# One pool for raw weights, split weights and activations; expert chunks split five ahead; the gated activation split half way through the next products

## The chip, the cores and the metric

The program runs as one launch on one core of a Trainium2 chip. The core has four compute engines with their own instruction queues, TensorE (PE, with its weight loads shown apart as PEld), VectorE (DVE), ScalarE (ACT) and GpSimd (POOL), a queue engine SyncE (SP) that issues the loads here, and DMA engines that move the data. The metric is the device time of the launch in microseconds (us).

## The reference

A two-layer encoder over 256 frames of width 1024, in float32. Each layer adds a token mixer (a convolution of 31 taps, a gated convolution of 3 taps, a spatial gating block), a cross-attention to 256 memory tokens, and a feed-forward: dense in layer 0, a mixture of experts in layer 1. Cut to the last, which takes most of the time:

```python
def moe_swiglu(xn, w_router, w_gate, w_up, w_down):
    xt = xn.reshape(-1, d)                                   # 256 tokens
    top_vals, top_idx = lax.top_k((xt @ w_router), 2)        # 2 of 8 experts
    top_w = jax.nn.softmax(top_vals, axis=-1)
    combine = jnp.sum(one_hot(top_idx, 8) * top_w[..., None], axis=1)
    for e in range(8):                                       # 1024 -> 3584 -> 1024
        y = y + combine[:, e:e + 1] * (silu(xt @ w_gate[e]) * (xt @ w_up[e])) @ w_down[e]
```

A final RMS norm follows.

## The kernel before

**Products in float32 by parts.** A weight is loaded as float32 (a *raw* tile `w`, 128x2048, 1 MiB, called a chunk here) and split: ACT copies it to a tile `hi` of the type that PE multiplies fast (L195), DVE subtracts to get the rest `lo` (L196). Activations are split in the same way, and a product is the sum of three: hi with hi, hi with lo, lo with hi (`mm3`, L216). The class `Stream` (L149) holds the sequence of chunks. `get` (L203) hands out the next split half-chunk; before that it splits as far ahead as `SPLIT_AHEAD = 3` half-chunks and `SPLIT_BUFS = 3` chunks allow, and each split issues the load of the chunk `ahead` places on. In the expert stage `wide` is set, and a whole chunk is split by one ACT and one DVE instruction. With these numbers, when PE is handed chunk k, chunk k+2 is split.

**The pools.** Tiles `hi` and `lo` come from a pool `hp` of 3 buffers each. Raw chunks and the large activations come from a pool `rp` of `R_BUFS = 16` buffers of 8 KB per partition; the expert stage loads `R_BUFS - 7 = 9` chunks ahead of the split (L1378). Small tiles come from `mp`. A buffer is written again when its last reader is done.

**The order.** Each engine runs its instructions in the order in which the code emits them. Buffers are assigned when the program is built.

**The expert stage** (`moe`, `Run.blocks`, `Block`). The experts are sorted by their number of tokens: eight places, four *large* (128 token slots) and four *small* (64 slots). A place has 7 blocks of 512 hidden columns, 56 blocks in all. `merged` (L1325) puts three large blocks first, then small and large in turn 25 times, then three small ones. A block has two chunks for the gate product, two for the value product and two for the down product, 336 chunks in all. A chunk takes 12 matmuls of 512 columns in a large block (all three products), 8 in a small one (hi and lo of the 64 slots share one 128-wide weight). For each block `b` and the block `prev` before it, `Run.blocks` emits:

1. `b.gate()`: two chunks, then ACT reads the result (a large block: Silu, L1235; a small one: a copy, L1213).
2. `prev.hidden()`: PE turns the gated activation of the block before (L1225 large, L1223 small); for a small block DVE multiplies gate and value (L1256); then ACT and DVE split it into `hl` (L1262, L1263).
3. `b.value()`: two chunks, then DVE multiplies by the gate (large, L1243) or ACT copies (small).
4. `b.gated()`: for a small block PE turns the gate and ACT takes the Silu (L1249).
5. `prev.down()`: two chunks against `hl` of the block before (PE tile `acc`; the gate and value products are PE tile `mm` from `xg`).

So from one small block's down product to the next there are 12 chunks: small down 2, small gate 2, small value 2, large down 2, large gate 2, large value 2. Such a stretch is called a pair here. Between these, `pe_later` works off the gathering of the next place's tokens (L1146) and the adding of a finished place to the residual (L1175 to L1177).

**Kept chunks.** In layer 1 the first products of the attention's keys are done from chunks that were loaded and split during the dense feed-forward of layer 0 (`KEPT = 2`, `keep_load`, `keep_split`); each holds two blocks of 1024 columns. The last two key blocks are multiplied unsplit in float32 (L460).

Of the kernel before, what the change touches and what calls it, by code (L numbers as in the profile page):

```python
# [21 lines left out]
F32R = mybir.dt.float32r  # L22
# [40 lines left out]
SPL = [(j * 512, min(512, FF - j * 512)) for j in range((FF + 511) // 512)]  # L63


KEPT = 2

R_BUFS = 16
M_BUFS = 8

SPLIT_BUFS = 3
SPLIT_AHEAD = 3

HALF = 64
SMALL = 4
# [5 lines left out]
def trunk(tc, x, xt_in, mem, mt_in, wa, wb, wc, wl0, wk1, wl1, wff, wmoe, cc, tk, moec, ident_d, gfin, out):  # L81
    nc = tc.nc
    PE, ACT, DVE, POOL = nc.tensor, nc.scalar, nc.vector, nc.gpsimd
    with contextlib.ExitStack() as c:
# [1 line left out]
        cp = c.enter_context(tc.tile_pool(name="cp", bufs=1))  # L86
        rp = c.enter_context(tc.tile_pool(name="rp", bufs=R_BUFS))
        mp = c.enter_context(tc.tile_pool(name="mp", bufs=M_BUFS))
        hp = c.enter_context(tc.tile_pool(name="hp", bufs=SPLIT_BUFS))
        sp = c.enter_context(tc.tile_pool(name="sp", bufs=SMALL_BUFS))  # L90
        pp = c.enter_context(tc.tile_pool(name="pp", bufs=8, space=bass.MemoryType.PSUM))
        n_ = [0]
# [1 line left out]
        def nm(s):  # L94
            n_[0] += 1
            return f"{s}{n_[0]}"
# [52 lines left out]
        class Stream:  # L149
# [28 lines left out]
            def do_split(self):  # L178

                c, j, w, full = self.parts[self.ns]  # L180
                self.dma(c + 1)
                if full:
                    self.split[self.ns] = self.raw[c][:, j * w:(j + 1) * w]
                    self.ns += 1
                    self.dma(c + self.ahead)
                    return
                n = len(self.src[c][2])
                if c not in self.tiles:
                    self.tiles = {c: (hp.tile([P, n * w], F32R, name=nm("hi"), tag="hi"),
                                      hp.tile([P, n * w], F32R, name=nm("lo"), tag="lo"))}  # L190
                hi, lo = self.tiles[c]
                m = n - j if self.wide else 1
                ws = slice(j * w, (j + m) * w)
                r = self.raw[c][:, ws]
                ACT.activation(hi[:, ws], r, AF.Copy)  # L195
                DVE.tensor_tensor(lo[:, ws], r, hi[:, ws].bitcast(F32), op=OP.subtract)  # L196
                for i in range(j, j + m):
                    ws = slice(i * w, (i + 1) * w)
                    self.split[self.ns] = hi[:, ws], lo[:, ws]
                    self.ns += 1  # L200
                self.dma(c + self.ahead)

            def get(self, held=0):  # L203

                i = self.i
                c0 = self.parts[i - held][0]
                while (self.ns < min(i + 1 + SPLIT_AHEAD, len(self.parts))
                       and self.parts[self.ns][0] < c0 + SPLIT_BUFS):
                    self.do_split()
                self.i += 1  # L210
                return self.split.pop(i)
# [627 lines left out]
        def up(st, s, accs, mid=None):  # L839


            np_ = s.w // 128
            per = 1024 // s.w

            def part(i, wh, wl, t):
                for j in range(per):
                    k = i * per + j
                    w = slice(j * s.w, (j + 1) * s.w)
                    a, b = s.x(k, t)
                    mm3(accs[t][:, 0:s.w], a, b, wh[:, w], wl[:, w], k == 0, k == KC - 1)  # L850

            if mid:
                parts = st.many(np_)
                for t in range(NT):
                    for i in range(np_):
                        part(i, *parts[i], t)
                        if t == 0 and i == np_ // 2 - 1:
                            mid()
            else:
                for i in range(np_):  # L860
                    w = st.get()
                    for t in range(NT):
                        part(i, *w, t)
# [322 lines left out]
        class Block:  # L1186
# [13 lines left out]
                for i, (a, w) in enumerate(ops):  # L1200
                    PE.matmul(out, a, w, start=first and i == 0, stop=last and i == len(ops) - 1)  # L1201

            def up(self, out):
                for c in range(2):
                    items = []
                    for i, (wh, wl) in enumerate(self.st.many(2)):
                        items += [(4 * c + 2 * i + q, wh[:, q * 512:(q + 1) * 512], wl[:, q * 512:(q + 1) * 512])
                                  for q in range(2)]
                    self.product(self.place.xg, out, items, c == 0, c == 1)
# [24 lines left out]
                    self.a = M([P, 512], s="a")  # L1234
                    ACT.activation(self.a, g, AF.Silu)  # L1235

            def value(self):
                u = mm()
                self.up(u)
                if self.small:  # L1240
                    self.u = self.copy(u)
                else:
                    DVE.tensor_tensor(self.a, u, self.a, op=OP.mult)  # L1243
# [5 lines left out]
                    ACT.activation(self.a, ps, AF.Silu)  # L1249

            def hidden(self):
                n = self.place.n
                if self.small:
                    ps = self.turn(self.u)
                    self.hl = M([P, 4, 2, n], F32R, s="hl")
                    DVE.tensor_tensor(self.a, ps, self.a, op=OP.mult)  # L1256
                    v = self.a.rearrange("p (f s) -> p f s", f=4)
                else:
                    v = self.turn(self.a).rearrange("p (f s) -> p f s", f=4)
                    self.hl = R([P, 4, 2, n], F32R, s="hl")  # L1260
                hi, lo = self.hl[:, :, 0], self.hl[:, :, 1]
                ACT.activation(hi, v, AF.Copy)  # L1262
                DVE.tensor_tensor(lo, v, hi.bitcast(F32), op=OP.subtract)  # L1263
# [18 lines left out]
        class Run:  # L1282
# [14 lines left out]
            def blocks(self, st, steps, before):  # L1297

                fin = Final()
                prev = None  # L1300
                todo = [Block(st, p, j) for p, j in steps]
                for i, b in enumerate(todo):
                    last = i == len(todo) - 1
                    if i in before:
                        before[i]()
                    if last:
                        fin.load()
                    b.gate()
                    pe_later()
                    if prev:  # L1310
                        prev.hidden()
                    pe_later()
                    b.value()
                    pe_later()
                    b.gated()
                    if prev:
                        prev.down(b.hidden if last else None)
                    pe_later()
                    prev = b
                while later:  # L1320
                    pe_later()
                table(AF.Sqrt)
                prev.down(end=lambda: fin.all(prev.place.part))
# [35 lines left out]
        def moe(st, routed, weights, sort, combine):  # L1359
            slot, comb, slotp, combp, which, bases, nmax, r, saved = routed  # L1360
            where["tile"] = which
            order = merged()
            run = Run(slotp, combp, r, saved)
            places = [Place(run, p, 1 <= p <= SMALL) for p in range(NE)]

            places[0].run = Run(slot, comb, r, saved)
            st.wide = True
            first = places[0].gather()
            later.append(first.pop())
            later.append(combine)  # L1370
            for i, f in enumerate(first):
                f()
                if i == 0:
                    for _ in range(2):
                        st.do_split()
                    weights()
                    sort()
            st.ahead = R_BUFS - 7  # L1378
            before = {}
            at = {x: i for i, x in enumerate(order)}  # L1380

            def add(i, f):
                before.setdefault(i, []).append(f)
            add(LEAD, run.save)
            for p in range(1, NE):
                add(max(1, at[p, 0] - 3), places[p].prepare)
            run.blocks(st, [(places[p], j) for p, j in order],
                       {i: lambda fs=fs: [f() for f in fs] for i, fs in before.items()})

        def moe_rest(routed):  # L1390

            slot, comb, slotp, combp, which, bases, nmax, r, saved = routed
            here = T([P, NT, NE])
            DVE.tensor_tensor(here, slot, bases.unsqueeze(1).to_broadcast([P, NT, NE]), op=OP.subtract)
            run = Run(here, comb, r, saved)
            places = [Place(run, p, False) for p in range(NE)]
            order = [(p, j) for p in range(NE) for j in range(NJ)]
            st = Stream(chunks(order, lambda p, i: wmoe[p, i]), R_BUFS - 7)
            st.wide = True
            for f in places[0].gather():  # L1400
                f()
            run.blocks(st, [(places[p], j) for p, j in order],
                       {NJ * p - 1: places[p].prepare for p in range(1, NE)})
# [55 lines left out]
        norm = mixer(1, st, kv1, norm, start1)  # L1459
        nxt = Norm(1, C_FFN, split=False)  # L1460
        attention(1, st, kv1, norm, nxt)
        st.ahead = R_BUFS - 2
        routed, *pieces = route(nxt)
        moe(st, routed, *pieces)

# [147 lines left out]
```

## Time and profile before

| | |
|---|---|
| Median of 3 runs | 1571.79 us (1569.81 to 1572.13) |
| Profiled execution | 1567.52 us, span of its instructions 1565.7 us |
| PE busy | 1499.6 us (96%) |
| PEld busy | 1252.6 us (80%) |
| DVE busy | 1300.0 us (83%) |
| ACT busy | 1053.0 us (67%) |
| Data moved | 459.03 MB, mean 293 GB/s |

The expert stage takes the time from about 590 us to the end: 336 of the loads, 347 GB/s over that stretch. Before it PE is busy for 581.04 of 590 us. A busy share of PE is not a share at its peak: matmuls follow each other closer than one takes, and their ends are modelled, so short waits between two matmuls stand within the busy time. They are seen from the starts in a timeline.

### The profile page before, as it was taken

What the parts mean: (1) busy time and instruction counts of PE and PEld (TensorE: products, weight loads), DVE (VectorE), ACT (ScalarE), POOL (GpSimd) and SP (SyncE); (2) the same over time, 40 slices, a digit from 0 to 9 for tenths busy, and PEclk for the clock granted to TensorE, in tenths of its full rate; (3) what the DMA queues carried; (4) which work ended last, traced back from release to release, by engine and by line L of the source; (5) the groups of instructions that cost most, each with busy time, mean ns of one, the idle gap of its engine ahead of it and who ended that gap; (6) DMA issues with size and microseconds to landing.
All of it is one profiled execution on the core that took longest, in us unless ns stands there. A gap on an engine that the chain in (4) does not pass through costs nothing.

```text
span 1565.7 us, 20799 instructions
## 1 busy us (share of the span) xinstructions
PE 1499.6 (96%) x7757; PEld 1252.6 (80%) x7757; DVE 1300.0 (83%) x1496; ACT 1053.0 (67%) x1224; POOL 8.1 (1%) x23
## 2 busy tenths in 40 slices
PE   7999999999999998999999999999999999999995
PEld 7998988888998997777777777877777877777773
DVE  7988676645888767988998998898998898998896
ACT  6547465543653655877777877787877787877784
POOL 0000000000000001000000000000000000000000
PEclk9999999999999999999999999999999999999998
DMA  9527644353443683899898999898999898999970
GB/s 375 202 108 280 238 183 161 138 211 125 158 187 135 242 323 143 312 385 402 345 386 312 389 389 403 353 381 333 368 385 409 349 389 329 376 381 404 400 308 30
DMA packets 65325, 459.03 MB, mean 293 GB/s; under 512 B 7232, under 2 KB 7744, under 8 KB 11840
## 3 DMA queue, kind: packets, MB, share of 16 engines
q1 hardware_dynamic: 65216, 457.62, 74.5%
q8 instruction: 63, 1.03, 0.3%
q14 instruction: 46, 0.38, 0.1%
HBM read 456.55 MB, written 1.05 MB: 292 GB/s over the span
## 4 chain that ended last, share of the span: by engine, by line
PE 59%; DVE 20%; DMA 9%; issue 7%; ACT 3%; SPq 0%; DVEq 0%; ACTq 0%
DVE lo L196 17%; PE mm L1201 12%; DMA w<-in_wmoe_dram 9%; PE acc L1201 8%; PE mm L219 5%; PE mm L217 5%; PE mm L218 5%; PE acc L218 3%; PE acc L219 3%; PE acc L217 3%; PE mm L460 2%; ACT hi L195 2%; PE z L218 2%; PE z L219 2%; PE z L217 2%
## 5 line engine op out<-in xcount | busy, mean ns | idle before, releaser
L196 DVE TENSOR_TENSOR lo<-w,hi 128x2048 fp32r<-128x2048 f32 (+3 forms) x504 | 946.5, 1914 | 122.0 <-ACT hi L195 116.6
L195 ACT ACTIVATE hi<-w 128x2048 fp32r<-128x2048 f32 (+3 forms) x504 | 793.3, 1614 | 179.9 <-PE acc L1201 57.1
L1201 PE MATMUL mm<-hi,xg 128*128 128x512 f32 x1344 | 410.3, 393 | 2.9 <-ACT xg L275 1.7
L1201 PE MATMUL mm<-lo,xg 128*128 128x512 f32 x896 | 305.3, 401 | 10.5 <-DVE lo L196 7.3
L1201 PEld LDWEIGHTS mm<-hi,xg 128*128 128x128 f32 x1344 | 250.6, 188 | 54.5 <-ACT xg L275 1.9
L1201 PEld LDWEIGHTS mm<-lo,xg 128*128 128x128 f32 x896 | 161.8, 188 | 74.6 <-DVE lo L196 45.7
L1201 PE MATMUL acc<-hi,hl 128*128 128x512 f32 x672 | 215.3, 395 | 1.9 <-DVE hl L1263 1.3
L1201 PE MATMUL acc<-lo,hl 128*128 128x512 f32 x448 | 163.4, 405 | 26.1 <-DVE lo L196 24.1
L1201 PEld LDWEIGHTS acc<-hi,hl 128*128 128x128 f32 x672 | 125.8, 188 | 28.1 <-DVE hl L1263 1.7
L1201 PEld LDWEIGHTS acc<-lo,hl 128*128 128x128 f32 x448 | 80.3, 188 | 63.5 <-DVE lo L196 50.0
L217 PE MATMUL z<-hi,xt 128*128 128x320 f32 (+1 forms) x256 | 78.3, 306 | 8.3 <-ACT xt L335 8.3
L218 PE MATMUL z<-lo,xt 128*128 128x320 f32 (+1 forms) x256 | 77.4, 302 | 0.3 <-DVE lo L196 0.3
L219 PE MATMUL z<-hi,xt 128*128 128x320 f32 (+1 forms) x256 | 77.5, 303 | 0.0
L545 DVE SCALAR_TENSOR_TENSOR ca<-ca,cct 128x256 f32<-128x256 f32 x180 | 77.0, 479 | 0.2
L217 PE MATMUL mm<-hi,xt 128*128 128x512 f32 (+1 forms) x192 | 71.8, 374 | 0.0
L219 PE MATMUL mm<-hi,xt 128*128 128x512 f32 (+1 forms) x192 | 71.4, 372 | 0.0
L218 PE MATMUL mm<-lo,xt 128*128 128x512 f32 (+1 forms) x192 | 71.3, 371 | 0.0
L1223 PEld LDWEIGHTS mm<-twice,gu 128*128 128x128 f32 x448 | 58.2, 191 | 4.1
L1223 PE MATMUL mm<-twice,gu 128*128 128x64 f32 x448 | 56.1, 268 | 0.0
L217 PEld LDWEIGHTS z<-hi,xt 128*128 128x128 f32 x256 | 49.2, 192 | 8.3 <-ACT xt L335 8.3
L1213 ACT ACTIVATE gu<-mm 128x512 f32<-128x512 f32 x56 | 33.4, 596 | 32.1 <-PE mm L1201 32.1
L218 PEld LDWEIGHTS z<-lo,xt 128*128 128x128 f32 x256 | 49.3, 193 | 0.5 <-DVE lo L196 0.5
(284 smaller groups left out, 1895.7 us busy)
## 6 DMA issues: line engine op xcount, KB each, us to landing
w<-in_wmoe_dram SPq DMA_DIRECT2D x336, 1024.0 KB, 7.4
w<-in_wl_dram SPq DMA_DIRECT2D x39, 1024.0 KB, 6.9
w<-in_wff_dram SPq DMA_DIRECT2D x33, 1024.0 KB, 4.9
w<-in_wb_dram SPq DMA_DIRECT2D x8, 960.0 KB, 8.6
w<-in_wa_dram SPq DMA_DIRECT2D x5, 1024.0 KB, 7.8
w<-in_wc_dram SPq DMA_DIRECT2D x8, 640.0 KB, 11.2
tk<-in_tk_dram SPq DMA_DIRECT2D x2, 1024.0 KB, 11.0
mt<-in_mem_t_dram SPq DMA_DIRECT2D x2, 1024.0 KB, 12.1
```

What stands on the lines that cost most here:

```text
L195: ACT.activation(hi[:, ws], r, AF.Copy)
L196: DVE.tensor_tensor(lo[:, ws], r, hi[:, ws].bitcast(F32), op=OP.subtract)
L217: PE.matmul(ps, ah, bh, start=start, stop=False)
L218: PE.matmul(ps, ah, bl, start=False, stop=False)
L219: PE.matmul(ps, al, bh, start=False, stop=stop)
L460: PE.matmul(self.kps[:, d, :], w[:, ks], self.mt[:, k, :], start=k == 0, stop=k == KC - 1)
L545: return lambda: DVE.scalar_tensor_tensor(dst, src[:, k:k + S], w, dst, op0=OP.mult, op1=OP.add)
L1201: PE.matmul(out, a, w, start=first and i == 0, stop=last and i == len(ops) - 1)
L1213: ACT.activation(m, ps, AF.Copy)
L1223: PE.matmul(ps[:, f * n:(f + 1) * n], w, twice, start=True, stop=True)
```

## The change

Pool `hp` goes; `hi` and `lo` come from `rp`, which grows from 16 to 22 buffers, so the memory stays the same. In the expert stage the split runs up to 8 half-chunks and 5 chunks ahead (`WIDE_AHEAD`, `WIDE_BUFS`): when PE is handed chunk k, chunk k+4 is split. The stage loads 7 chunks ahead of the split in place of 9 (`WIDE_LOAD`). At the entry to the stage the load goes 14 ahead in both versions (`R_BUFS - 2` before, `6 * LEAD - 4` now). Outside the stage the numbers of the split stay at 3. The split of the gated activation into `hl` leaves `hidden` and becomes `parts`, which is called between the two chunks of the next block's value product. `KEPT` goes from 2 to 3: one chunk more of layer 1 is loaded and split during layer 0's feed-forward, and with it the two key blocks that were multiplied unsplit become split products of three matmuls.

```diff
-KEPT = 2
-
-R_BUFS = 16
+KEPT = 3
+
+R_BUFS = 22
 M_BUFS = 8
-SPLIT_BUFS = 3
-SPLIT_AHEAD = 3
+SPLIT_BUFS, SPLIT_AHEAD = 3, 3
+WIDE_BUFS, WIDE_AHEAD = 5, 8
+
+WIDE_LOAD = 7
...
-        hp = c.enter_context(tc.tile_pool(name="hp", bufs=SPLIT_BUFS))
...
                 if c not in self.tiles:
-                    self.tiles = {c: (hp.tile([P, n * w], F32R, name=nm("hi"), tag="hi"),
-                                      hp.tile([P, n * w], F32R, name=nm("lo"), tag="lo"))}
+                    self.tiles = {c: (R([P, n * w], F32R, s="hi"),
+                                      R([P, n * w], F32R, s="lo"))}
...
-                while (self.ns < min(i + 1 + SPLIT_AHEAD, len(self.parts))
-                       and self.parts[self.ns][0] < c0 + SPLIT_BUFS):
+                ahead, bufs = (WIDE_AHEAD, WIDE_BUFS) if self.wide else (SPLIT_AHEAD, SPLIT_BUFS)
+                while self.ns < min(i + 1 + ahead, len(self.parts)) and self.parts[self.ns][0] < c0 + bufs:
                     self.do_split()
...
-            def up(self, out):
+            def up(self, out, mid=None):
                 for c in range(2):
+                    if c and mid:
+                        mid()
...
             def hidden(self):
+                if self.small:
+                    DVE.tensor_tensor(self.a, self.turn(self.u), self.a, op=OP.mult)
+                else:
+                    self.a = self.turn(self.a)
+
+            def parts(self):
                 n = self.place.n
-                if self.small:
-                    ps = self.turn(self.u)
-                    self.hl = M([P, 4, 2, n], F32R, s="hl")
-                    DVE.tensor_tensor(self.a, ps, self.a, op=OP.mult)
-                    v = self.a.rearrange("p (f s) -> p f s", f=4)
-                else:
-                    v = self.turn(self.a).rearrange("p (f s) -> p f s", f=4)
-                    self.hl = R([P, 4, 2, n], F32R, s="hl")
+                self.hl = (M if self.small else R)([P, 4, 2, n], F32R, s="hl")
+                v = self.a.rearrange("p (f s) -> p f s", f=4)
                 hi, lo = self.hl[:, :, 0], self.hl[:, :, 1]
                 ACT.activation(hi, v, AF.Copy)
                 DVE.tensor_tensor(lo, v, hi.bitcast(F32), op=OP.subtract)
...
-                    b.value()
+                    b.value(prev and prev.parts)
                     pe_later()
                     b.gated()
+
+                    def hidden():
+                        b.hidden()
+                        b.parts()
                     if prev:
-                        prev.down(b.hidden if last else None)
+                        prev.down(hidden if last else None)
...
-            st.ahead = R_BUFS - 7
+            st.ahead = WIDE_LOAD
...
-        st.ahead = R_BUFS - 2
+        st.ahead = 6 * LEAD - 4
```

First place: DVE in the expert stage, from the multiply of a large block's value product by its gate (`a`) to the split of that activation into `hl`, while PE works on the small blocks beside it. Each `lo` from `w` and `hi` is the split of one chunk. Before:

```order
L1243 TENSOR_TENSOR a_6324<-mm_6335,a_6324 128x512
L196 TENSOR_TENSOR lo_6376<-w_6218,hi_6375 128x2048
L196 TENSOR_TENSOR lo_6390<-w_6232,hi_6389 128x2048
L196 TENSOR_TENSOR lo_6405<-w_6255,hi_6404 128x2048
L196 TENSOR_TENSOR lo_6419<-w_6273,hi_6418 128x2048
L1263 TENSOR_TENSOR hl_6439<-mm_6434,hl_6439 128x4x128
L196 TENSOR_TENSOR lo_6444<-w_6292,hi_6443 128x2048
```

After (all line numbers are some lines on):

```order
L1246 TENSOR_TENSOR a_6367<-mm_6375,a_6367 128x512
L197 TENSOR_TENSOR lo_6419<-w_6298,hi_6418 128x2048
L197 TENSOR_TENSOR lo_6433<-w_6316,hi_6432 128x2048
L197 TENSOR_TENSOR lo_6448<-w_6335,hi_6447 128x2048
L197 TENSOR_TENSOR lo_6462<-w_6353,hi_6461 128x2048
L197 TENSOR_TENSOR lo_6484<-w_6380,hi_6483 128x2048
L1266 TENSOR_TENSOR hl_6497<-mm_6477,hl_6497 128x4x128
L197 TENSOR_TENSOR lo_6501<-w_6401,hi_6500 128x2048
```

Four chunk splits stood between the two, now five do: the split of `hl` has moved from behind the small block's gate chunks to between its two value chunks, and each split is of a chunk two places further on.

Second place: ACT in the same stage, from a large block's Silu (`a` from `mm`) to the copy for the small block's `hl` that follows; each `hi` from `w` is the copy of one chunk. Before:

```order
L195 ACTIVATE hi_6535<-w_6393 128x2048
L1235 ACTIVATE a_6553<-mm_6516 128x512
L1262 ACTIVATE hl_6560<-a_6478 128x4x64
L195 ACTIVATE hi_6565<-w_6408 128x2048
L195 ACTIVATE hi_6583<-w_6422 128x2048
```

After:

```order
L196 ACTIVATE hi_6578<-w_6465 128x2048
L1238 ACTIVATE a_6596<-mm_6559 128x512
L196 ACTIVATE hi_6605<-w_6487 128x2048
L1265 ACTIVATE hl_6623<-a_6521 128x4x64
L196 ACTIVATE hi_6626<-w_6504 128x2048
```

The copy of a chunk now stands between the Silu and the copy of `hl`, which before followed the Silu at once.

## Rows read from the trace of the kernel before

**Rows 1.** Stretches: length; busy PE, PEld, DVE, ACT, POOL; clock, DMA share, GB/s.

```profile
883.70:918.50 34.80, 32.97 (x149) 25.73 (x148) 32.33 (x23) 26.28 (x20) 0.00 (x0) 1.00 0.95 371
918.50:950.40 31.90, 31.04 (x141) 24.32 (x140) 28.77 (x17) 25.09 (x18) 0.00 (x0) 1.00 0.99 402
982.30:1017.60 35.30, 34.52 (x175) 28.19 (x174) 31.89 (x29) 27.54 (x27) 0.00 (x0) 1.00 0.87 345
1017.60:1050.90 33.30, 32.41 (x147) 25.44 (x146) 31.64 (x22) 26.24 (x21) 0.00 (x0) 1.00 0.99 390
1050.90:1087.30 36.40, 35.16 (x177) 28.39 (x176) 29.97 (x30) 25.44 (x27) 0.00 (x0) 1.00 0.93 360
1087.30:1121.10 33.80, 31.34 (x141) 24.38 (x141) 30.64 (x17) 26.91 (x19) 0.00 (x0) 1.00 0.85 336
883.70:1121.10 237.40, 228.43 (x1065) 180.77 (x1064) 213.98 (x149) 182.59 (x148) 0.00 (x0) 1.00 0.94 371
1489.10:1550.20 61.10, 53.73 (x245) 40.70 (x244) 54.27 (x37) 45.26 (x38) 0.00 (x0) 1.00 0.46 186
```

**Rows 2.** Who waited for whom, 640 to 1500 us: total us, times, longest.

```profile
PEld mm L1201 <- DVE lo L196: 43.5, 79, 0.8
PEld acc L1201 <- DVE lo L196: 42.4, 69, 2.0
...
ACT hi L195 <- DMA w<-in_wmoe_dram: 4.8, 6, 0.8
```

**Rows 3.** The load queue's own waits, 640 to 1500 us.

```profile
SPq L169 <- DVE lo L196: 586.3, 246, 10.0
```

**Rows 4.** Chain of work that ended last, in order of time: start, us, what.

```profile
470.17 6.91 PE mm L460 x32
...
938.79 2.73 PE mm L1201 x12
```

**Rows 5.** Timeline of PE, 918 to 934 us: start, us, instructions, idle before.

```profile
918.53 0.62 PE L1201 MATMUL acc<-hi,hl 128*128 128x512 f32 x2
...
927.13 0.60 PE L1225 MATMUL mm<-ident,a 128*128 128x128 f32 x4
927.48 1.18 PE L1201 MATMUL mm<-hi,xg 128*128 128x512 f32 x4
...
931.53 1.00 PE L1223 MATMUL mm<-twice,gu 128*128 128x64 f32 x8
932.34 0.48 PE L1201 MATMUL acc<-hi,hl 128*128 128x512 f32 x1
933.30 0.50 PE L1201 MATMUL acc<-lo,hl 128*128 128x512 f32 x1 [0.48 <-DVE lo L196]
```

**Rows 6.** Timeline of DVE, 914 to 931 us.

```profile
914.73 0.43 DVE L1263 TENSOR_TENSOR hl<-a,hl 128x256 fp32r<-128x256 f32 x1 [0.48 <-ACT hl L1262]
916.54 4.49 DVE L196 TENSOR_TENSOR lo<-w,hi 128x2048 fp32r<-128x2048 f32 x2 [1.38 <-ACT hi L195]
920.95 0.69 DVE L1243 TENSOR_TENSOR a<-mm,a 128x512 f32<-128x512 f32 x1
921.55 8.89 DVE L196 TENSOR_TENSOR lo<-w,hi 128x2048 fp32r<-128x2048 f32 x4
930.36 0.69 DVE L1263 TENSOR_TENSOR hl<-mm,hl 128x512 fp32r<-128x512 f32 x1
```

**Rows 7.** Timeline of ACT, 912 to 919 us.

```profile
912.39 0.60 ACT L1235 ACTIVATE a<-mm 128x512 f32<-128x512 f32 x1 [0.80 <-PE mm L1201]
...
914.61 3.71 ACT L195 ACTIVATE hi<-w 128x2048 fp32r<-128x2048 f32 x2
```

**Rows 8.** The page, DMA issues: line, count, KB each, median us to landing.

```profile
w<-in_wmoe_dram SPq DMA_DIRECT2D x336, 1024.0 KB, 7.4
```

**Rows 9.** Timeline of PE in the second layer, 456 to 459 us.

```profile
456.99 0.28 PE L217 MATMUL mm<-ms,khi 128*128 128x256 f32 x1
...
458.06 0.28 PE L217 MATMUL mm<-ms,khi 128*128 128x256 f32 x1
```

More of the change, by code (lines that the diff above doesn't have):

```diff
@@ L1235, in gate, with value @@
                     ACT.activation(self.a, g, AF.Silu)
-            def value(self):
+            def value(self, mid=None):
                 u = mm()
-                self.up(u)
+                self.up(u, mid)
                 if self.small:
@@ L1397, in moe_rest @@
             order = [(p, j) for p in range(NE) for j in range(NJ)]
-            st = Stream(chunks(order, lambda p, i: wmoe[p, i]), R_BUFS - 7)
+            st = Stream(chunks(order, lambda p, i: wmoe[p, i]), WIDE_LOAD)
             st.wide = True
```

## The prediction

> **What bounds the kernel now.** I read the busy shares first, then the busy times by stretch, then the waits, then the timelines of PE and DVE over one pair. PE is busy for nearly all of the span, so the first question is whether that busy time holds waits. The stretches [rows 1] show the expert stage as a repeating cycle: seven pairs in 237.4 us, with PE busy 228.43, DVE 213.98, ACT 182.59, and DMA at a share of 0.94. Three resources stand near their limits, and none is at it. The waits [rows 2] say who holds whom: PE's weight loads waited for the rests `lo` of chunks 148 times, 85.9 us in sum, while ACT waited for a landing 4.8 us in all. The load queue waits for DVE to free buffers, 586.3 us [rows 3]. So loads are not late; PE waits for splits.
>
> How much it loses is read from the starts. A chunk of a large block takes 2.73 us for 12 matmuls [rows 4], 0.2275 us each. In the pair of [rows 5] the small block's down product starts at 918.53 and the large block's at 932.34: 13.81 us. In between stand 6 small chunks, 48 matmuls or 10.92 us, the turn of the large activation (927.13 to 927.48, 0.35) and that of the small one (931.53 to 932.34, 0.81), 12.08 in sum. So 1.73 us are waits. Then the first matmul with a rest starts at 933.30, 0.96 after the one before in place of 0.23: 0.73 more. That is 2.5 us of a steady pair of 31.9 [rows 1]. The rest, 31.9 - 13.81 - 0.73 = 17.36 us, is the large half, which I take as free of waits.
>
> The cause is DVE. In the small half a chunk lasts PE 1.82 us and DVE 2.2 (four from 921.55 to 930.36 [rows 6]); with three buffers DVE can't start a chunk before PE has left the chunk three back, and it sat idle for 1.38 us just before, at 916.54.
>
> **The change part by part.** *Five chunks of split.* DVE may go two chunks further ahead in the large half, where PE is the slower one. I follow one pair through the new order. ACT's Silu ends at 912.39 + 0.60 = 912.99 [rows 7]; the copy of the chunk takes 1.85 (3.71 for two), to 914.8; DVE subtracts until 917.0; `hl` of the small block follows (0.43 at 914.73 [rows 6]), until 917.5. The next chunk needs a buffer that PE leaves at the end of the large block's first value chunk, 918.53 - 2.73 = 915.8; its copy is done at 917.7 and its rest at 919.9. There the multiply by the gate starts, against 920.95 before. Then come five splits, not four: 919.9 + 0.6 + 5 x 2.2 + 0.69 = 932.2 for the end of `hl`. PE, no longer held in the small half, would reach the large down product at 918.53 + 12.08 = 930.61 and needs the rest of `hl` at the third matmul, 931.06. So the wait does not vanish: about 1.2 us stay, now for `hl` and not for a chunk. A steady pair goes from 31.9 to 12.08 + 1.2 + 17.36 = 30.6 us.
>
> This rests on when the multiply starts. It can't start before PE has ended the value product, 918.6 (then `hl` ends at 930.9, and nothing is left to wait for: 2.5 us gained), and if it starts as late as before, at 920.95, `hl` ends at 933.2 and the third matmul is where it was: nothing gained. I take 919.9, the value nearest to what the rows give step by step: the two waits that came before it (DVE idle for 0.48 and 1.38 us, at 914.73 and 916.54 [rows 6]) lose their cause, ACT's Silu at 912.39 does not.
>
> *The other pairs.* Where a place ends or a new one is gathered, DVE or PE has more to do, and I take the larger need of the two in each pair. PE's need is its busy time less 1.6 us, since the steady pair shows 31.04 busy for 31.9 - 2.5 = 29.4 of need. By [rows 1], in order of time: 32.3 (DVE), two steady pairs of 29.4 (the second has no row of its own), 32.9 (PE), 31.6 (DVE), 33.6 (PE), 30.6 (DVE): 219.8. With 1.2 us of wait in each of seven, 228.2, against 237.4: 9.2 us a cycle. The stretch from the first small down product to the last but three holds 24 pairs (25 small blocks alternate with large ones), or 3.43 cycles: 31.5 us.
>
> *The ends of the stage.* The three large blocks at the head have chunks slower than DVE: I count 1 us there. From 1489.10 to 1550.20 small blocks dominate and DVE is busy 54.27 of 61.10 us [rows 1]; of its 6.8 us idle I take 4.5, because waits for buffers go but the chain of the last block stays.
>
> *Loads seven ahead, and buffers shared.* Seven before the split and four after it are 11 chunks before PE, against 9 and 2 before: the same. But a raw chunk now often lies where a half was, and so waits for PE: in the built program, of 300 chunks in the middle, 189 raw tiles follow a `hi` or `lo` of ten or eleven chunks earlier, 86 a raw chunk of seven to nine earlier. Ten chunks of PE are some 25 us (ten twelfths of a pair), and a load lands 7.4 us after its issue [rows 8], so I cost it at nothing. Without that cover the load comes late, and the second rival prices what loads at their limit leave.
>
> The Trainium skill speaks against this: "DMA: Bandwidth & Descriptors", section Specifications, gives about 358 GB/s of HBM for a core and a ceiling of 435 GB/s; worked out from these as estimates, the 12.58 MB of a pair take 35.1 us by the first, and the loads would be the bound already and nothing gained; by the second they take 28.9 us. The trace has 402 GB/s in a steady pair [rows 1], above the first figure, so I do not go by it.
>
> *`hl` half way.* Besides its place in DVE's queue, above, it takes the stop of ACT for DVE's multiply out of the small `hl`. Its price, one more split in front, is in the 1.2 us.
>
> *Kept chunks.* The two key blocks, 6.91 us as 32 float32 matmul instructions [rows 4], become 48 of 0.119 (456.99 to 458.06 for nine [rows 9]), 5.7: 1.2 us less. One more load and two splits on ACT and DVE go to the dense stage of layer 0, beside PE, which is the busy engine there (581.04 of the first 590 us, as the profile section says); on the path they would be a chunk's 2.2 us on DVE. Six buffers are then held until the keys are made, so loads of the second mixer start later; I see no wait there now and count none.
>
> *Sum.* 31.5 + 1 + 4.5 + 1.2 = 38. The profiled execution took 1567.52 us (1565.7 of span, 1.8 around it) and becomes 1529.5. It lies 4.3 below the median of the runs; on that scale 1571.79 - 38 = 1533.8, which I round to 1533.
>
> **The rivals.** *PE stops waiting altogether.* If DVE's lead carries over from pair to pair, a cycle needs PE's 31.4 + 2 x 29.4 + 32.9 + 30.8 + 33.6 + 29.7 = 217.2: 20.2 less, 69 over the stage, 77 with the ends: 1495. Against it: DVE's 213.98 of busy time would then be a share of 0.985.
>
> *The transfers become the bound.* Taking each pair's DMA share as its need [rows 1]: 33.1, 31.6 twice, 30.7, 33.0, 33.9, 28.7. With the needs above where these are larger (32.9 and 30.6), and 1.2 us of wait in those two, 229.1: 8.3 a cycle, 28.5 us over the stage, 1537 with the ends. The share of 0.99 in the steady pair speaks for it; against it, that ACT waited only 4.8 us for landings [rows 2] and that the queue waits for buffers, not the buffers for it [rows 3].
>
> *The wait only changes its name.* DVE reaches the multiply as late as now, at 920.95, and five splits stand before `hl`: nothing gained in the pairs, the ends stay too; 1570.
>
> *`hl` comes too late.* With halves and raw chunks in one pool, a split can meet a buffer that frees one chunk later than in a ring of its own. Then one more split of 2.2 us falls behind PE, and the wait at the large down product is 3.4 us in place of 2.5: 0.9 x 24 = 22 us slower, 1592. It decides when `hl` ends later than 933.2 on the clock of [rows 6], 14.7 us after the small down product starts.
>
> **How the numbers follow.** Forecast 0.63 (its own range 1517 to 1550), no more waits 0.09, transfers 0.08, change of name 0.09, too late 0.11. Faster by over 0.2% (some 3 us, about what can be told from no change) is the first three, 0.80; the fourth lies within it but for its edges, 0.08; slower is the last and the upper edge of the fourth, 0.12. The range 1505 to 1572 leaves out the first and the last rival.
>
> **What would show it.** Right: waits of PE for `lo` within the small chunks gone, a wait for `hl` on DVE at the large down product of about 1 us, a steady pair of 30 to 31 us, a cycle near 228, DVE idle less. Wrong: a pair still near 31.9 with the wait at `hl` (the name has changed); waits of ACT for landings well over 4.8 us (transfers); gaps in DVE for buffers in the large half, with `hl` past 14.7 us (too late); PE idle in the second mixer before 600 us (kept chunks).

## The result and the profile after

The changed kernel takes 1521.28 us (median of 4 runs, 1520.13 to 1523.26), the kernel before 1571.96 (median of 4 beside it): a ratio of 0.9682, 95% interval 0.9665 to 0.9699, 50.7 us less. The forecast was 1533, its own range 1517 to 1550. The span of the profiled execution fell from 1565.7 to 1518.4 us, by 47.3.

First the stretches of the changed kernel, cut at the same places of the program as [rows 1] (length; busy PE, PEld, DVE, ACT, POOL; clock, DMA share, GB/s): the pair in which a place ends, the first steady pair, the pair before the last of the cycle, the cycle of seven, and the last stretch.

```profile
871.30:904.57 33.27, 31.63 (x150) 26.13 (x148) 32.23 (x23) 25.94 (x21) 0.00 (x0) 1.00 0.94 375
904.57:934.87 30.30, 29.79 (x142) 24.62 (x140) 28.47 (x17) 24.74 (x19) 0.00 (x0) 1.00 1.00 412
...
1031.49:1066.27 34.78, 34.15 (x177) 28.56 (x175) 30.38 (x31) 26.65 (x28) 0.00 (x0) 1.00 0.89 360
871.30:1097.60 226.30, 220.12 (x1066) 182.87 (x1065) 212.62 (x149) 180.94 (x149) 0.00 (x0) 1.00 0.96 390
1449.60:1510.00 60.40, 52.62 (x253) 43.03 (x251) 53.56 (x47) 43.51 (x46) 0.00 (x0) 1.00 0.57 235
```

The steady pair went from 31.9 to 30.30 us, the cycle from 237.4 to 226.3. PE's busy time fell with it (228.43 to 220.12 for the same matmuls): what left was waiting inside the busy time. By the starts of the small down products, the 24 pairs took 771.3 us (678.3 to 1449.6) after 808.0, 36.7 less; the stretch before them gave 2.8 (it began at 681.1), the end, from the start of the last full pair, took 68.8 us after 76.6, 7.8 less. These are the 47.3.

Who waits for whom in the expert stage of the changed kernel, 640 to 1500 us (total us, times, longest), against [rows 2]:

```profile
ACT a L1238 <- PE mm L1202: 58.9, 26, 3.5
PEld acc L1202 <- DVE hl L1266: 36.0, 31, 2.1
DVE lo L197 <- ACT hi L196: 29.5, 34, 1.7
ACT hi L196 <- PE mm L1202: 27.2, 30, 2.3
PE acc L1202 <- DVE hl L1266: 23.2, 27, 1.8
ACT hi L196 <- DVE lo L197: 23.0, 35, 1.3
```

PE's 148 waits for `lo` are gone; what it waits for now is `hl` at the large down product. ACT waits for PE before the Silu: it has run ahead. No wait of ACT for a landing is listed, though from issue to landing a chunk now takes 7.9 us in the median, after 7.4 [rows 8]. The load queue's own waits, which stood on DVE for 586.3 us [rows 3], now stand on PE, since raw chunks lie where halves were:

```profile
SPq L170 <- PE mm L1202: 367.0, 133, 8.0
SPq L170 <- PE acc L1202: 187.9, 89, 7.0
SPq L170 <- DVE lo L197: 79.2, 55, 4.3
```

The timeline of DVE over the steady pair from 904.57 answers to [rows 6] (start, us, instructions, idle before and who ended it):

```profile
905.60 0.68 DVE L1246 TENSOR_TENSOR a<-mm,a 128x512 f32<-128x512 f32 x1
906.20 11.09 DVE L197 TENSOR_TENSOR lo<-w,hi 128x2048 fp32r<-128x2048 f32 x5
917.21 0.68 DVE L1266 TENSOR_TENSOR hl<-mm,hl 128x512 fp32r<-128x512 f32 x1
917.81 11.09 DVE L197 TENSOR_TENSOR lo<-w,hi 128x2048 fp32r<-128x2048 f32 x5
929.56 0.42 DVE L1256 TENSOR_TENSOR a<-mm,a 128x256 f32<-128x256 f32 x1 [0.66 <-PE mm L1226]
931.15 2.29 DVE L197 TENSOR_TENSOR lo<-w,hi 128x2048 fp32r<-128x2048 f32 x1 [1.17 <-ACT hi L196]
933.36 0.42 DVE L1266 TENSOR_TENSOR hl<-a,hl 128x256 fp32r<-128x256 f32 x1
```

The multiply by the gate starts 1.03 us after the small down product (it was 2.42, 920.95 against 918.53), five splits follow, and `hl` ends at 917.89. The small `hl` at 933.36 has no wait in front of it or behind it; [rows 6] had 0.48 us and 1.38 there. DVE still idles as long, 0.66 and 1.17 us (1.83 against 1.86), but now because it has run ahead of PE: the multiply at 929.56 waits for PE's turn, and the split at 931.15 for a copy that stands in ACT behind a Silu which itself waited for PE's gate product (below). PE meets `hl` at its third matmul, as the timeline of PE has it, against [rows 5]:

```profile
916.73 0.48 PE L1202 MATMUL acc<-hi,hl 128*128 128x512 f32 x1
917.04 0.40 PE L1202 MATMUL acc<-lo,hl 128*128 128x512 f32 x1
917.95 0.73 PE L1202 MATMUL acc<-hi,hl 128*128 128x512 f32 x2 [0.51 <-DVE hl L1266]
```

From 917.04 to 917.95 are 0.91 us in place of 0.23. DVE's multiply no longer holds ACT there. Before, between the Silu's end (912.99) and the next copies [rows 7], ACT stood still for it:

```profile
914.28 0.42 ACT L1262 ACTIVATE hl<-a 128x256 fp32r<-128x256 f32 x1 [1.30 <-DVE a L1256]
```

In the changed kernel the copy for the small `hl` follows a chunk's copy without idling; what ACT waits for now is PE, in front of the Silu:

```profile
928.72 0.60 ACT L1238 ACTIVATE a<-mm 128x512 f32<-128x512 f32 x1 [2.67 <-PE mm L1202]
929.21 1.91 ACT L196 ACTIVATE hi<-w 128x2048 fp32r<-128x2048 f32 x1
931.02 0.40 ACT L1265 ACTIVATE hl<-a 128x256 fp32r<-128x256 f32 x1
```

The wait of PE for `hl` is nearly all that is left in the pair (some 0.9 of 1.1 us of stall, by the starts of all matmuls; 2.7 before).

### The profile page after: what moved, and what is told of

Read it like the earlier page. It is cut to its first block, busy times and chain, and to the rows that moved or that the text cites. A ratio compares the mean times of both kernels' runs of the same rounds, so it can differ in the third digit from the quotient of the medians.

```text
span 1518.4 us, 20836 instructions
## 1 busy us (share of the span) xinstructions
PE 1468.9 (97%) x7773; PEld 1263.6 (83%) x7773; DVE 1295.8 (85%) x1498; ACT 1046.9 (69%) x1226; POOL 8.0 (1%) x23
## 3 DMA queue, kind: packets, MB, share of 16 engines
q8 instruction: 63, 1.03, 0.3%
## 4 chain that ended last, share of the span: by engine, by line
PE 83%; DVE 8%; ACT 4%; issue 3%; DMA 0%; SPq 0%; DVEq 0%; ACTq 0%
PE mm L1202 26%; PE acc L1202 16%; PE mm L220 5%; PE mm L218 5%; PE mm L219 5%; DVE lo L197 5%; PE acc L219 3%; PE acc L220 3%; PE acc L218 3%; ACT hi L196 3%; PE z L219 2%; PE z L220 2%; PE z L218 2%; PE mm L461 2%; PE mm L490 2%
## 5 line engine op out<-in xcount | busy, mean ns | idle before, releaser
L1202 PE MATMUL mm<-lo,xg 128*128 128x512 f32 x896 | 294.5, 390 | 0.0
L1202 PE MATMUL acc<-hi,hl 128*128 128x512 f32 x672 | 219.1, 401 | 23.5 <-DVE hl L1266 23.5
L1202 PEld LDWEIGHTS mm<-lo,xg 128*128 128x128 f32 x896 | 168.3, 188 | 34.6
L1202 PE MATMUL acc<-lo,hl 128*128 128x512 f32 x448 | 157.4, 392 | 0.0
L1202 PEld LDWEIGHTS acc<-lo,hl 128*128 128x128 f32 x448 | 84.6, 189 | 17.0
L1238 ACT ACTIVATE a<-mm 128x512 f32<-128x512 f32 x28 | 16.7, 596 | 61.3 <-PE mm L1202 61.3
```

## The experiments

Times are medians; "gain" is against the kernel before in the same set of runs (1567.98 us for the first four, 1569.95 for the second, 1569.42 for the third). The diffs are against the changed kernel; four experiments (e2, e5, e6, e9) edit the kernel before instead, and say so.

### First set: is it the lead, or the place of `hl`?

**The lead of before, all else as changed.**

```diff
-WIDE_BUFS, WIDE_AHEAD = 5, 8
-WIDE_LOAD = 7
+WIDE_BUFS, WIDE_AHEAD = 3, 3
+WIDE_LOAD = 9
```

> The changed kernel, but with three buffers and three parts of split lead for the wide chunks, as before (loads nine ahead in place of seven, so that as many chunks as after stand between landing and PE). hl stays half way, the one pool and the third kept chunk stay. My theory (depth makes the gain): the waits of PE for lo in the small chunks come back, a steady pair is 31.5 to 32 us, and the time is 1555 to 1572. Rival B (the place of hl makes the gain, since DVE no longer stops for ACT in front of it): steady pair 30.3 to 30.8, time 1520 to 1535. Rival C (the shared pool, the later load and the kept chunk make it): time 1520 to 1530 as well, but then the kernel e2_mid gains nothing, where B has it near 1530.

1520.45 us, ratio 0.9696 (0.9679 to 0.9713): no different from the changed kernel. My theory fell with its first run: given the rest of the change, the lead of five gives nothing. The steady pair is again 30.30 us.

**`hl` half way alone, on the kernel before** (`parts` called between the two chunks of the value product; pools, lead and loads untouched).

> The kernel before, with one part of the change: the split of hl half way through the next value product (pools, depth, loads and kept chunks as before). My theory: 1562 to 1573, steady pair 31.5 to 32, since PE still waits for lo of chunks that DVE can't start for want of a buffer. Rival B (place of hl): 1522 to 1540. Rival C (pool, loads, kept): 1568 to 1575.

1538.69 us, 0.9814 (0.9796 to 0.9832): 29.3 us of gain from this edit by itself, where my theory had at most 6; the time lies at the upper end of rival B's range.

**The changed kernel with `hl` back behind the turn.**

```diff
                     if prev:
                         prev.hidden()
+                        prev.parts()
                     pe_later()
-                    b.value(prev and prev.parts)
+                    b.value()
```

> The changed kernel, but hl split where it was before, right behind the turn, ahead of the value product's splits: four chunk splits stand between the multiply by the gate and the large hl, not five. My theory: the wait of PE at the large down product (0.9 us a pair) goes, as hl ends some 2.2 us earlier; the stop of DVE for ACT ahead of the small hl comes back and takes some 0.5 us of DVE a pair. DVE is busy 214 of the 226 us of seven pairs, so a part of the gain turns into waits for lo: steady pair 29.6 to 30.4, time 1500 to 1522. Rival B (place of hl made the gain): steady pair 31 or more, time 1540 to 1570.

1530.49 us, 0.9759 (0.9742 to 0.9777): 9.2 us slower than the changed kernel, between the two theories. The wait at the large down product shrank and didn't go: by the starts, PE's stalls within its first chunk are 27.6 us in 28 large blocks, against 32.9 in the changed kernel. DVE's timeline says why. From the split behind one small `hl` (903.74) to that behind the next (934.08) are 30.34 us, and in these DVE stands still only for ACT, 0.48 and 1.38 us (last two rows, [rows 6] had the same); its own work takes the rest, and behind the large `hl` it now has six splits to do, not five, before the small block's multiply, so the next multiply by the gate comes later than in the changed kernel.

```profile
903.74 4.50 DVE L197 TENSOR_TENSOR lo<-w,hi 128x2048 fp32r<-128x2048 f32 x2 [1.38 <-ACT hi L196]
908.15 0.68 DVE L1246 TENSOR_TENSOR a<-mm,a 128x512 f32<-128x512 f32 x1
908.75 8.89 DVE L197 TENSOR_TENSOR lo<-w,hi 128x2048 fp32r<-128x2048 f32 x4
917.56 0.69 DVE L1266 TENSOR_TENSOR hl<-mm,hl 128x512 fp32r<-128x512 f32 x1
918.16 13.30 DVE L197 TENSOR_TENSOR lo<-w,hi 128x2048 fp32r<-128x2048 f32 x6
931.36 0.42 DVE L1256 TENSOR_TENSOR a<-mm,a 128x256 f32<-128x256 f32 x1
932.27 0.43 DVE L1266 TENSOR_TENSOR hl<-a,hl 128x256 fp32r<-128x256 f32 x1 [0.48 <-ACT hl L1265]
934.08 2.29 DVE L197 TENSOR_TENSOR lo<-w,hi 128x2048 fp32r<-128x2048 f32 x1 [1.38 <-ACT hi L196]
```

The multiply starts 4.5 us after the small down product (903.65), and `hl` ends 14.6 after it, in spite of one split fewer. This pair follows one in which a place ends, and takes 31.60 us. In the next, by the starts, the multiply comes 3.24 us after, one split (2.2) later than in the changed kernel, and PE's stall is 0.9 and the pair 30.29 us, as there: what the missing split gives is taken by the later start. The loss lies in the other pairs, where DVE has more to do, and at the end: PE waits for DVE where a place is added and the next gathered, and the stretch from the start of the last full pair (1453.2) to the end takes 73.5 us, 4.7 more than in the changed kernel. The adding and the gathering have these rows in the waits, 640 to 1450 us:

```profile
PE mm L1177 <- DVE y L271: 4.1, 3, 1.4
PE mm L1147 <- DVE pg L1132: 3.5, 3, 1.3
```

**Mixed: a large block's `hl` behind its turn, a small block's half way.**

```diff
                     if prev:
                         prev.hidden()
+                        if not prev.small:
+                            prev.parts()
                     pe_later()
-                    b.value(prev and prev.parts)
+                    b.value(prev and prev.small and prev.parts)
```

> The changed kernel, but the large block's hl is split right behind its turn (four chunk splits in front, as before), and the small block's half way (as after). My theory: the wait at the large down product goes without the stop of DVE for ACT; cycle of seven pairs 219 to 223 in place of 226.3, time 1497 to 1512. Rival D (DVE is the limit by now: 859.87 us busy of the 928.4 of the expert stage): the wait moves to lo of a chunk, cycle 225 to 227, time 1517 to 1523.

1492.16 us, 0.9515 (0.9496 to 0.9533): 75.8 us of gain, below my range and 29 us better than the changed kernel. The stretches of its cycle and of a steady pair:

```profile
864.70:1083.00 218.30, 218.22 (x1065) 183.19 (x1064) 212.09 (x149) 181.35 (x148) 0.00 (x0) 1.00 0.99 405
896.20:925.80 29.60, 29.58 (x140) 24.80 (x141) 29.02 (x17) 24.74 (x18) 0.00 (x0) 1.00 1.00 414
```

And the same place in DVE's timeline, four splits in front of the large `hl`, no stop of 1.38 us behind the small one:

```profile
898.18 0.69 DVE L1246 TENSOR_TENSOR a<-mm,a 128x512 f32<-128x512 f32 x1
898.79 8.89 DVE L197 TENSOR_TENSOR lo<-w,hi 128x2048 fp32r<-128x2048 f32 x4
907.59 0.69 DVE L1266 TENSOR_TENSOR hl<-mm,hl 128x512 fp32r<-128x512 f32 x1
908.19 13.30 DVE L197 TENSOR_TENSOR lo<-w,hi 128x2048 fp32r<-128x2048 f32 x6
921.40 0.43 DVE L1256 TENSOR_TENSOR a<-mm,a 128x256 f32<-128x256 f32 x1
922.11 2.29 DVE L197 TENSOR_TENSOR lo<-w,hi 128x2048 fp32r<-128x2048 f32 x1 [0.29 <-ACT hi L196]
924.32 0.42 DVE L1266 TENSOR_TENSOR hl<-a,hl 128x256 fp32r<-128x256 f32 x1
```

The large down product starts at 908.50 there, and `hl` ends at 908.28: PE doesn't wait. So rival D fell too: DVE, busy 212.09 of 218.30 us, can run nearly without a gap.

### Second set: what in `hl` half way, and what without it?

The new theory came from two rows of before, the instructions of the `hl` lines by name (count, total and mean, idle of the engine just before), 680 to 1450 us:

```profile
L1263 DVE TENSOR_TENSOR hl<-a,hl 128x256 fp32r<-128x256 f32 x22 | 9.4, 426 | 10.7 <-ACT hl L1262 10.7
L1262 ACT ACTIVATE hl<-a 128x256 fp32r<-128x256 f32 x22 | 9.2, 419 | 33.1 <-DVE a L1256 33.1
```

ACT runs its instructions in the order of the code. Its copy for the small `hl` waits for DVE's multiply, 33.1 us in 22 pairs; in that time it copies no chunk, so that DVE, once past `hl`, waits 1.38 us more for a copy.

**Only the small block's `hl` half way, on the kernel before**, and **only the large block's.**

```diff
                         prev.hidden()
+                        if not prev.small:     # second kernel: if prev.small
+                            prev.parts()
                     pe_later()
-                    b.value(prev and prev.parts)
+                    b.value(prev and prev.small and prev.parts)   # not prev.small
```

(Against the kernel of e2.)

> The kernel before, with hl split half way for small blocks alone; a large block's hl is split right behind its turn, as before. Theory H, formed after the first four runs: the gain of hl half way comes from the small block, where ACT, which works in order, held its copy for hl until DVE's multiply (33.1 us of ACT idle in 22 pairs of the trace of before) and so had no copied chunk ready for DVE. By H 1520 to 1541 (e2_mid, both half way, took 1538.69; here the large hl has one split fewer in front). Rival L, it comes from the large block, whose hl no longer holds up the splits: 1560 to 1572.

> The kernel before, with hl split half way for large blocks alone; a small block's hl right behind its multiply, as before. By theory H no gain or a loss: 1564 to 1590, since ACT still waits for the small block's multiply and the large hl has one split more in front. By rival L 1535 to 1545.

Small: 1544.41 us, 0.9841 (0.9823 to 0.9859), 25.5 of gain, 3 us outside the range. Large: 1564.48, 0.9966 (0.9953 to 0.9978), 5.5 of gain. So most of the 29.3 comes from the small block, as the theory said; it had not seen the small gain of the large one.

**The one pool alone** (the changed kernel with the edits of e1 and of e3 together).

> The changed kernel with the lead of three parts and three buffers of before (loads nine ahead) and hl where it was before: what is left of the change is the one pool of 22 buffers and the third kept chunk. Theory P: what lets DVE run ahead is the buffer that a split waits for, and in the one pool that is free early whatever the lead; so the time is that of e3_early (1530.49) within 8 us, 1522 to 1540. Rival: the lead of five chunks is needed where hl isn't half way: 1555 to 1570.

1552.66 us, 0.9897 (0.9877 to 0.9916): 17.3 of gain, from the pool and the third kept chunk. It fits neither range: without `hl` half way the lead does matter, 22.2 us (1530.49 with it).

**Mixed with the lead of before** (e4 with the edit of e1).

> The kernel e4_mixed (small hl half way, large hl behind its turn, one pool) with the lead of three parts and three buffers, loads nine ahead. Theory P: the lead matters little, 1488 to 1500. Rival: with DVE this near its limit (0.95 of a cycle) the lead of five is needed, 1505 to 1520.

1524.51 us, 0.9713 (0.9695 to 0.9731): theory P fell, the lead is worth 32 us here, more than the rival had. Its waits (PE for `lo` at the down product) and the timeline of PE at the large down product show how:

```profile
PEld acc L1202 <- DVE lo L197: 21.5, 25, 1.7
```

```profile
919.27 0.47 PE L1202 MATMUL acc<-hi,hl 128*128 128x512 f32 x1
920.22 0.50 PE L1202 MATMUL acc<-lo,hl 128*128 128x512 f32 x1 [0.48 <-DVE lo L197]
```

`hl` is there, after four splits as in e4, but the chunk of the down product itself is not: with this lead its split stands behind `hl` in DVE's order, and PE needs it already at the second matmul.

### Third set: the hold of ACT, the kept chunk, the loads, one chunk of lead

**The first half of the small `hl` by DVE, on the kernel before**, its place unchanged.

```diff
-                ACT.activation(hi, v, AF.Copy)
+                if self.small:
+                    DVE.tensor_copy(out=hi, in_=v)
+                else:
+                    ACT.activation(hi, v, AF.Copy)
```

> The kernel before, with one thing changed: the first half of the small block's hl is made by DVE instead of ACT. Places, rings and lead as before. It tells what of the small block's place counts. Theory H (ACT, held in order by its copy for hl until DVE's multiply, has no copied chunk ready): that hold is gone, DVE no longer idles 0.48 and 1.38 us there, and pays some 0.3 us more work a pair; 1540 to 1556. Rival (it is the place of hl among DVE's splits that counts): no gain, DVE has more to do, 1566 to 1582.

1543.27 us, 0.9833 (0.9818 to 0.9848): 26.2 of gain, as much as e5, though DVE has more to do. Its timeline at the small `hl`:

```profile
939.06 0.42 DVE L1256 TENSOR_TENSOR a<-mm,a 128x256 f32<-128x256 f32 x1
939.51 0.29 DVE L1263 CAST hl<-a 128x256 fp32r<-128x256 f32 x1
939.84 0.43 DVE L1266 TENSOR_TENSOR hl<-a,hl 128x256 fp32r<-128x256 f32 x1
940.18 2.28 DVE L196 TENSOR_TENSOR lo<-w,hi 128x2048 fp32r<-128x2048 f32 x1
```

No gap: 0.3 us of work takes the place of 1.86 us of waiting. With e5 this shows the cause of the small block's part: it is ACT's hold, not the place of `hl` among DVE's splits.

**Two kept chunks in place of three**, and **loads four ahead of the split in place of seven.**

```diff
-KEPT = 3
+KEPT = 2
```

> The changed kernel with two kept chunks in place of three. The prediction gave the third 1.2 us: 1522 to 1524. Rival, that its load and splits cost what it saves: 1519.5 to 1521.5; then the first expert matmul starts no later than in the changed kernel (601.47 us).

```diff
-WIDE_LOAD = 7
+WIDE_LOAD = 4
```

> The changed kernel with loads four chunks ahead of the split in place of seven (eight chunks of PE ahead in place of eleven, some 20 us, against 7.9 us from issue to landing). The prediction's view that loads are hidden: no change, 1518 to 1524. Rival, transfers are near the bound (DMA share 0.91): ACT waits for landings, 1530 to 1560.

Kept: 1524.34 us, 0.9718 (0.9703 to 0.9733), 1.9 above e11 in the same set, 3.1 above the changed kernel in another. In the traces the first expert matmul starts at 602.89 us in place of 601.47 (1.42 later; the prediction had 1.2), so the rival fell, and the time is 0.3 above my range; the last block takes 1.6 us more, which I can't explain. The other traces say the same of the start: 601.3 to 602.0 us in the eight with three kept chunks, 602.5 to 603.3 in the six with two. Loads: 1522.48 us, 0.9706 (0.9689 to 0.9723), as expected, not told apart from the changed kernel's 0.9682 (0.9665 to 0.9699), though ACT now does wait for landings, in the waits from 640 to 1450 us:

```profile
ACT hi L196 <- DMA w<-in_wmoe_dram: 20.8, 42, 1.4
```

These waits lie on ACT while it is ahead; no cost shows in the time.

**Mixed with one chunk of lead less** (`WIDE_BUFS, WIDE_AHEAD = 4, 6`, `WIDE_LOAD = 8`).

> The kernel e4_mixed with one chunk less of lead (four buffers, six parts; loads eight ahead). Theory Q: what e8_mixed3 lacked is that the chunk of the large down product itself was split behind hl; with one chunk more of lead it stands in front, and nothing more is needed: 1490 to 1498. Rival, each chunk of lead counts: half way between e4 and e8, 1504 to 1514.

1493.64 us, 0.9516 (0.9501 to 0.9531): theory Q holds. One chunk over the lead of before puts the down product's own chunk in front of `hl` (e8 to e12, 31 us); the next one gives nothing (e4, 1492.16).

### The parts together

| `hl` of small / large | pool of before, lead of before | one pool, lead of before | one pool, lead of five |
|---|---|---|---|
| turn / turn | 1567.98 to 1571.96 | 1552.66 | 1530.49 |
| turn / half way | 1564.48 | not run | not run |
| half way / turn | 1544.41 | 1524.51 | 1492.16 |
| half way / half way | 1538.69 | 1520.45 | 1521.28 |

(The two columns of the one pool hold the third kept chunk too.) The parts don't add up: they take away the same idle time of DVE, which is busy 213.98 of the 237.4 us of a cycle before, 212.62 of 226.3 in the changed kernel and 212.09 of 218.30 in e4. And the bottom row shows why the change leaves 29 us: with both halves moved, five splits and `hl` stand between the multiply by the gate and the large down product, whatever the lead (in a steady pair `hl` ends 13.3 us after the small down product starts, in e1 as in the changed kernel). Five splits by 2.2 us and `hl` end 12.3 us after the multiply starts (905.60 to 917.89); four end after 10.1 (898.18 to 908.28, e4). With the lead of before, moving the large `hl` too gives 4 to 6 us instead (first and second column), since there the down product's own chunk is late. A lead of five with separate, larger pools was not run, so what the lead gives without the pool is open.

## Why the prediction was right, and where it was not

The sign and the new wait came out as forecast; 38 us of gain were forecast, 47.3 measured on the same scale (span against span).

- *The steady pair*: 30.6 forecast, 30.30 measured. The wait that stays, 1.2, is 0.7 at the matmul named (0.91 in place of 0.23) and 0.9 over that chunk. `hl` ends 13.3 us after the small down product starts (the forecast, 932.2, is 13.7), short of the 14.7 from which the last rival decides.
- *The start of the multiply*, on which it rested: 1.4 us after the small down product, measured 1.03. The chain that I followed (Silu, copy, split, `hl`, split, multiply) is the one in the timelines, but its wait for a buffer is not: the copies behind the small `hl` follow without a wait.
- *The other pairs*: 228.2 a cycle forecast, 226.3 measured. By kind: 33.5 against 33.27 for the pair where a place ends, 34.8 against 34.78 for [rows 1]'s 1050.90. Most of the shortfall is here: 36.7 us over 24 pairs, not 31.5.
- *The ends*: 4.5 forecast, 7.8 measured for the tail. Between the starts of the last three small down products, 17.24 and 7.97 us became 15.20 and 4.70. In e6 they are still 17.24 and 7.97, in e5 15.20 and 5.85: the small `hl`, whose stop of ACT comes at every block there, is what I had not priced.
- *The kept chunk*: 1.2 forecast; the first expert matmul starts 1.25 us earlier than in the kernel before, 1.42 earlier than in e10.
- *Loads*: nothing, and nothing lost (e11). The page cited from the Trainium skill did not decide; a steady pair now runs at 412 GB/s, after 402 [rows 1].

The step that failed is the one that says where the gain comes from. I laid it to "*Five chunks of split*", costed the shared buffers at nothing and gave `hl` half way no gain of its own. The runs showed otherwise: with `hl` half way in the one pool the lead of five gives 0 (e1; 22 and 32 us with the large `hl` behind its turn, e7 to e3 and e8 to e4); `hl` half way alone gives 29.3 (e2); the pool with the kept chunk gives 17 to 18 (e7; e2 to e1), some 15 of them the pool's. What I called the depth was in part the ring, the small pool whose buffers come round again after three chunks: in e1, with the lead of before, ACT's waits for PE to leave a `hi` buffer are 8.2 us (640 to 1450 us),

```profile
ACT hi L196 <- PE acc L1202: 8.2, 21, 1.1
```

against two rows of e2, which has the same lead and the same place of `hl` but the pools of before (in the kernel before they are 51.3 and 17.0),

```profile
ACT hi L195 <- PE acc L1201: 45.8, 46, 2.0
...
ACT hi L195 <- PE mm L1201: 29.5, 36, 1.5
```

since in a pool of 22 a buffer comes round later. That the pool's 15 us come from these waits is argued, not shown: in e4, the fastest, ACT runs further ahead and they are 69.2 us again.

That the time was still near is mostly the walk through one pair, which followed DVE and ACT, saw that both waits of [rows 6] go, and priced what is late next; it holds whichever edit takes them away. Which edit that was I read from the edit's name, not from who ended the wait; the row said ACT `hl`. Which edit the 5 us more in the other pairs come from, no run tells.

The first rival, PE not waiting at all, was right as a bound: 217.2 us a cycle, and e4 reached 218.30. Its gain of 77 is 76 by its own terms (69 + 1 + 4.5 + 1.2); e4 gained 75.8, at a busy share of DVE of 0.97, which I had taken as an argument against it.

## What to carry to other kernels

- An engine that works in order and stands between two streams holds both: before deepening a ring, look for a short instruction on the copying engine that waits for the engine it feeds (here 0.42 us of ACT, 33.1 us of waiting), and move that one, or give it to the engine that it waits for.
- A lead has to put the consumer's own next operand in front of the late item, and no more; count what stands in the queue between the release and the need (here four splits or five), for that number sets the wait, not the depth of the buffers.
- Of edits made together, test each alone and each left out, and halves of one too: here `hl` half way gives 29 us alone and 9 on top of the rest, and its part for the large block costs 29 where the rest is in place.

## What the runs showed of the hardware

- Over a steady pair of e4 a core's loads ran at 414 GB/s with a DMA share of 1.00, and landed 8.7 us after their issue in the median, while no wait of ACT for a landing shows among its waits: with loads issued some eleven chunks ahead of PE, engines that are busy all the time were late for nothing. The Trainium skill ("DMA: Bandwidth & Descriptors", Specifications) has about 358 GB/s of HBM for a core and a ceiling of 435; the trace goes past the first and stays under the second.
- ACT stood still for 33.1 us in front of 22 short copies, with copies of chunks behind them in its order; where DVE made those halves (e9), it copied on. The Trainium skill ("PSUM — Partial Sum Buffer", Engine vs sequencer instructions) calls ScalarE's queue a strict FIFO; the trace agrees.
